# A hybrid encoder step on one core: two more gate pairs as products of halves, a written engine order ahead of them, sample logits in split products, and mask and maximum as one operation

## The chip, the cores and the metric

The kernel runs on one core of a Trainium2 chip. The metric is device time of one execution in microseconds (us). Engines are named as in the profile: PE (TensorE) multiplies matrices, PEld is its weight load, DVE (VectorE), ACT (ScalarE) and POOL (GpSimd) work element by element, SP (SyncE) issues most DMAs; ACT issues some. "Granted clock" is the share of TensorE's full clock that it got.

## What is computed

One step of a one-layer encoder with two parallel branches, for a prompt of 1024 tokens and a sample of 64 tokens that continues 128 cached ones. The model width is 1024, with 16 heads of 64. Cut to what matters here:

```python
z = rms_norm(x, g_pre) @ w_in          # x path, gate, q, k, v, gate, forget logits, two merge gates
xa, ga, q, k, v, gb, fl, ma, mb = jnp.split(z, ...)
ya = rg_lru(causal_conv(xa, ...), ...) * silu(ga)
logf = log_sigmoid(fl + b_f); cum = cumsum(logf)
s = einsum('qhd,khd->hqk', q, k) * HEAD_DIM ** -0.5 + cq - ck      # ck, cq: running sums of logf
p = softmax(where(kpos <= qpos, s, -inf))
yb = einsum('hqk,khd->qhd', p, v) * silu(gb)
mix = sum(sigmoid([ma, mb]) * [ya @ w_branch[0], yb @ w_branch[1]]) @ w_o
h = x + rms_norm(mix, g_post)
y = h + rms_norm(sigmoid(h @ w_ple_gate) * (pe @ w_ple_proj), g_ple)
```

Outputs are y, the new k, v and logf, and the recurrent states, for prompt and sample. Everything is float32.

## The kernel before

**Split products.** A float32 product is made of three matmuls in the format `float32r` (a rounded float32): each operand is split into a high part (a copy by ACT, `copy_act`, L80) and a low part (what is left, `sub`, L83, on DVE or POOL), and `three` (L166 to L169) adds high by high, high by low and low by high. The sample's scores and values in attention are made of plain float32 matmuls instead.

**Gate panels.** z is made of panels of 128 columns, transposed: `panel_steps` takes a panel in three chunks of 364, 364 and 360 tokens, each of eight steps (one per 128 rows of the contraction) of three matmuls, into one of two accumulators of the pool `mm`. A chunk ends with `spill`: ACT copies the accumulator to SBUF and issues the write to DRAM (L269). The queue `gates` holds 24 panels: ma, mb and gb, eight each. `fetch` (L236) issues a panel's weights on SP, `split_next` splits them, `panel` hands out the next and looks ahead by one.

**The stages, in order.**

1. Norm, transposes, v and the forget logits, in nine token blocks (to L518).
2. Two plain panels (`PLAIN = 2`), while ACT and DVE make the split sums and differences T1 to T4 of the quarters of the normed input (`split_sum`). They are used by
3. ten pairs (`quads`, function `seven`): two panels of weights are taken as a 2 x 2 matrix of quarters and multiplied by the quarters of the input in seven products instead of eight, in the manner of Strassen and Winograd (L691). `split_pair` makes the sums of weights (POOL) and splits them (ACT, DVE); `put` brings results out. Eight pairs are k and q of a pair of heads, two are x and gate panels of the recurrent branch (kind "r": results go to DRAM as they are). Between products, `between` runs a step of `running_sums` (cumulative logf, softplus of the decay) or writes keys out (`keys_out`).
4. Attention (from L828). Scores (L990, L991) of 128 queries against up to 1024 keys go to one of two PSUM tiles, `s1` for up to 512 keys and `s2` for more, one buffer each. `softmax` adds the causal mask to the last 128 columns (DVE, L968), takes the negated maximum (DVE, L970), the exponential with its sum (ACT, L972), the reciprocal (DVE, L974) and scales (POOL, L975). `turn` transposes the probabilities (PE, L1012) and splits them (ACT, DVE); `values` multiplies by v (L1036, L1037). Per pair of heads the sample does the same once (`sample_keys`, `sample_scores` L1066 to L1068, `sample_turn`, `sample_values`); its inputs come by `load_sample` (L951 to L960), v by `load_v` (L930).
5. The recurrent branch, the branch and output projections, the last norm and gate.

**What sets the order.** PE follows the program's order throughout (`tc.manual_schedule`). ACT, DVE and POOL are ordered by the framework's scheduler, except in the opening, in attention and in the recurrent branch, where the program's order holds for them too. In attention that order is made by a small planner: a clock `now` in ns runs along PE's work (`spent`), each operation of ACT, DVE and POOL is booked at a time with a cost (`book`, constants at L36 to L40), and a step of scores, turns or values is taken when its inputs are due plus `SLACK` = 600 ns; if none is, one step of a gate panel fills the gap (`filler`, `book_split` books its weight split 5000 ns after the panel's start). What gate panels are left when attention is done run alone behind it.

## Time and profile before

| what | value |
|---|---|
| median of 3 runs | 1516.44 us (1512.67 to 1519.98) |
| profiled execution, its own time | 1513.6 us |
| its span, first to last instruction | 1511.9 us |
| mean granted clock of TensorE | 0.988 |
| bytes moved by DMA | 181.74 MB, 120 GB/s |

A row of the groups of instructions reads: line, engine, operation, written from read tile, partitions x elements, xcount, then busy us and mean ns of one, then the idle time before them and what ended it. A row in order of time reads: start, duration (us), engine, line, operation, count. A row of the waits reads: engine, tile and line that waited, what it waited for, us in total, times, longest.

### The profile page before, as it was taken

The page shows a single profiled execution, that of the slowest core. Times are in us where ns is not written, and L with a number is a line of the kernel's source. Part 1 is how long each engine was busy: PE and PEld are TensorE (multiplying, and loading weights), DVE is VectorE, ACT ScalarE, POOL GpSimd, SP SyncE. Part 2 cuts the span into 40 slices and gives each one's busy share as a digit, 9 for nine tenths or more (in the row PEclk, how much of TensorE's full clock was granted, in tenths as well). Part 3 has the DMA queues.
Part 4 walks back from the last instruction along what each step waited for, and adds up shares of the span by engine and source line. Part 5 has one row for each costly group of instructions (what it writes and reads, how often), then busy time and mean ns, then how long its engine had stood idle before and what let it go on. Part 6 is the DMA issues. An engine that isn't in the chain of part 4 may idle for free.

```text
span 1511.9 us, 25944 instructions
## 1 busy us (share of the span) xinstructions
PE 1462.3 (97%) x10064; PEld 1435.2 (95%) x10064; DVE 891.2 (59%) x1490; ACT 688.0 (46%) x1350; POOL 345.8 (23%) x416
## 2 busy tenths in 40 slices
PE   7999999999899999999999999989999999999998
PEld 6998999999899999999999999989999999999997
DVE  5463756644166766766676236999855554337644
ACT  4423434432155565656565325566544333324533
POOL 4010414312123322322332003556323000000001
PEclk9999999999999999999999999999999999999999
DMA  5344355553665546455451331111278544215111
GB/s 192 112 119 97 114 162 179 170 155 124 187 153 123 152 105 153 116 130 130 119 133 51 99 89 44 53 34 43 66 248 267 180 145 134 84 31 169 57 48 42
DMA packets 172951, 181.74 MB, mean 120 GB/s; under 512 B 21516, under 2 KB 148700, under 8 KB 172828
## 3 DMA queue, kind: packets, MB, share of 16 engines
q1 hardware_dynamic: 153724, 153.30, 36.7%
q10 hardware_dynamic: 19104, 26.79, 5.0%
q8 instruction: 79, 1.29, 0.4%
q14 instruction: 44, 0.36, 0.1%
HBM read 122.11 MB, written 57.93 MB: 119 GB/s over the span
## 4 chain that ended last, share of the span: by engine, by line
PE 64%; DVE 6%; ACT 3%; DMA 1%; issue 1%; POOL 1%; DVEq 0%; SPq 0%; POOLq 0%; ACTq 0%
PE acc L167 14%; PE acc L169 14%; PE acc L168 14%; PE tp L1012 4%; PE quad L691 3%; PE pv L1036 3%; PE pv L1037 3%; PE s L990 2%; PE s L991 2%; DVE u L1283 1%; DMA d_gb<-st 1%; DVE e_e L1342 1%; DVE e L1342 1%; PE tp L1636 1%; PE acc7p L169 1%
## 5 line engine op out<-in xcount | busy, mean ns | idle before, releaser
L169 PE MATMUL acc<-xh,wl 128*128 128x364 f32 (+1 forms) x864 | 286.4, 332 | 6.9 <-DVE wl L83 6.9
L167 PE MATMUL acc<-xh,wh 128*128 128x364 f32 (+1 forms) x864 | 287.0, 332 | 3.5 <-ACT st L80 3.5
L168 PE MATMUL acc<-xl,wh 128*128 128x364 f32 (+1 forms) x864 | 285.8, 331 | 0.0
L169 PEld LDWEIGHTS acc<-xh,wl 128*128 128x128 f32 x864 | 164.6, 190 | 7.5 <-DVE wl L83 7.5
L167 PEld LDWEIGHTS acc<-xh,wh 128*128 128x128 f32 x864 | 165.2, 191 | 4.7 <-ACT st L80 4.1
L168 PEld LDWEIGHTS acc<-xl,wh 128*128 128x128 f32 x864 | 164.7, 191 | 0.4
L83 DVE TENSOR_TENSOR wl<-wraw,wh 128x1024 fp32r<-128x1024 f32 (+1 forms) x82 | 96.6, 1177 | 109.7 <-ACT wh L80 109.3
L80 ACT ACTIVATE wh<-wraw 128x1024 fp32r<-128x1024 f32 (+1 forms) x82 | 77.8, 949 | 91.8 <-PE quad L691 44.4
L975 POOL TENSOR_SCALAR pb<-pb,sm 128x896 f32<-128x896 f32 (+1 forms) x64 | 61.6, 963 | 192.8 <-DVE sm L974 188.9
L970 DVE TENSOR_REDUCE nm<-s 128x1 f32<-128x128 f32 (+8 forms) x136 | 99.6, 732 | 3.8
L80 ACT ACTIVATE th<-tp 128x512 fp32r<-128x512 f32 x96 | 56.1, 594 | 51.5 <-PE tp L1012 47.9
L83 DVE TENSOR_TENSOR tl<-tp,th 128x512 fp32r<-128x512 f32 x96 | 65.3, 687 | 17.0 <-ACT th L80 16.0
L990 PE MATMUL s<-k,q 128*128 128x256 f32 (+1 forms) x192 | 66.5, 350 | 8.1 <-ACT pm L972 8.1
L80 ACT ACTIVATE st<-acc 128x364 f32<-128x364 f32 (+1 forms) x72 | 33.8, 471 | 87.9 <-PE acc L169 67.1
L167 PE MATMUL acc<-wqh,hth 128*128 128x256 f32 x256 | 73.1, 285 | 0.0
L167 PE MATMUL acc<-wqh,mxh 128*128 128x256 f32 x256 | 72.6, 283 | 0.0
L168 PE MATMUL acc<-wql,mxh 128*128 128x256 f32 x256 | 72.5, 283 | 0.0
L168 PE MATMUL acc<-wql,hth 128*128 128x256 f32 x256 | 72.5, 283 | 0.0
L169 PE MATMUL acc<-wqh,mxl 128*128 128x256 f32 x256 | 72.5, 283 | 0.0
L169 PE MATMUL acc<-wqh,htl 128*128 128x256 f32 x256 | 72.5, 283 | 0.0
L972 ACT ACTIVATE pb<-s,nm 128x896 f32<-128x896 f32 (+1 forms) x64 | 61.0, 954 | 18.8 <-DVE nm L970 10.1
L691 PE MATMUL quad<-xh,wh 128*128 128x272 f32 x320 | 68.3, 295 | 0.4 <-ACT p__3650 L80 0.4
(506 smaller groups left out, 4171.5 us busy)
## 6 DMA issues: line engine op xcount, KB each, us to landing
wraw<-in_w_in SPq DMA_DIRECT2D x58, 512.0 KB
q<-d_q SPq DMA_DIRECT2D x48, 256.0 KB
k<-d_k SPq DMA_DIRECT2D x48, 256.0 KB
wraw<-in_w_branch SPq DMA_DIRECT2D x16, 512.0 KB
gate<-d_ma SPq DMA_DIRECT2D x8, 544.0 KB
yb_in<-d_y SPq DMA_DIRECT2D x8, 544.0 KB
gb_in<-d_gb SPq DMA_DIRECT2D x8, 544.0 KB
gate<-d_mb SPq DMA_DIRECT2D x8, 544.0 KB
```

Source lines behind the costliest of these rows:

```text
L80: act.activation(out=out, in_=in_, func=AF.Copy, scale=scale)
L83: return eng.tensor_tensor(out=out, in0=in0, in1=in1, op=ALU.subtract)
L167: pe.matmul(out, ah, bh, start=start, stop=False)
L168: pe.matmul(out, ah, bl, start=False, stop=False)
L169: pe.matmul(out, al, bh, start=False, stop=stop)
L691: pe.matmul(acc[:, c, :CW], l[:, k, :], r[:, k, c * CW:(c + 1) * CW], start=(first and k == 0 and p == 0), stop=(k == 3 and p == 2), skip_ ...
L970: at = book("D", at - HOP, per(D_MAX, n), lambda: dve.tensor_reduce(out=nm, in_=s[:, :n], axis=AX.X, op=ALU.max, negate=True))
L972: free = book("A", at, per(A_EXP, n), lambda: act.activation(out=pr[:, :n], in_=s[:, :n], func=AF.Exp, bias=nm, accum_out=sm))
L975: return free, book("G", at, per(G_NORM, n), lambda: pool.tensor_scalar(out=pr[:, :n], in0=pr[:, :n], scalar1=sm, scalar2=1.0, op0=ALU.mul ...
L990: pe.matmul(s[:, c0:c0 + w], t["q1"][:, q0:q0 + P], t["k1"][:, c0:c0 + w], start=True, stop=False)
L1012: pe.transpose(tp[:, o0 + i * P:o0 + (i + 1) * P], pr[par][:, kb * P:(kb + 1) * P], ident[:, :])
L1036: pe.matmul(pv[:, :256], v, th[:, c], start=(g == 0 and j == 0), stop=False)
```

## The change

- `MORE = 2`: the last four panels of `gates` (gb 4 to 7) are taken off the queue and become two more pairs of kind "r", twelve pairs in all. 18 panels stay for attention's fill instead of 22. The weights of even pairs are loaded into `wpool`, those of odd pairs into `sp_`, the other way round than before.
- Ahead of the pairs ACT and DVE follow a written order: the chunks of the two plain panels, halves of the splits T2 and T4, and the parts of the first pair's split alternate. The first operations of `running_sums` are pinned to their place in the program.
- The sample's k and q parts are written as high and low parts like the prompt's (`put`, tensors `d_k`, `d_q` of T columns) and its scores are three `float32r` matmuls and a fourth, of six rows, for all running-sum terms (`cs_q`, `cs_k`), instead of three float32 ones.
- `softmax`: mask and maximum are one DVE operation over all columns (`tensor_tensor_reduce`); it writes the negated masked scores back to PSUM. The mask tile becomes 128 x 1024, zero but for its last 128 columns, and moves from the constants to attention's pool.
- `load_v` loads and splits half a pair's values at a time; the planner's costs follow.

```diff
@@ constants and queues
+MORE = 2
-D_MASK, D_MAX, D_INV, ... = (100.0, 1.35), (155.0, 1.045), 160.0, ...
+D_MAX, D_INV, ... = (240.0, 1.05), 160.0, ...
+    some += [gates.pop() for _ in range(2 * MORE)]
-    quads += [[(src, ("r", dst)) for src, dst in some[i:i + 2]] for i in (0, 2)]
+    quads += [[(src, ("r", dst)) for src, dst in some[i:i + 2]] for i in range(0, len(some), 2)]
+    n_gates = len(gates)
...
+    def split_half(x, t, j):
+        x_, h_, l_ = (halves(y)[j] for y in (x, *t))
+        copy_act(h_, x_)
+        sub(dve, l_, x_, f(h_))
...
+        elif b == NBLK - 1:
+            plain_1 = panel()
...
-    split_sum(rc, *T3)
-    whole(rc, 1, 0)
-    sub(dve, rc, rc, ra)
-    split_sum(ra, *T2)
-    split_sum(rc, *T4)
-    r23.close()
...
-        pl = (sp_, wpool)[i % 2]
+        pl = (wpool, sp_)[i % 2]
...
+    seq = tc.manual_schedule(engines={act.engine, dve.engine})
+    seq.__enter__()
+    steps = gate_panel(*plain_1)
+    chunk(steps)
+    split_sum(rc, *T3)
+    whole(rc, 1, 0)
+    sub(dve, rc, rc, ra)
+    split_half(ra, T2, 0)
+    chunk(steps)
+    split_half(ra, T2, 1)
+    plain_2 = panel()
+    split_half(rc, T4, 0)
+    run(steps)
+    split_half(rc, T4, 1)
+    r23.close()
...
     first_split = split_pair(0, pairs[0], first_w)
-    steps = gate_panel()
-    for i in range(3 * KT):
-        next(steps)
-        if i in (7, 15):
-            next(first_split)
+    steps = gate_panel(*plain_2)
+    next(first_split)
+    chunk(steps)
+    next(first_split)
+    chunk(steps)
+    next(first_split)
     run(steps)
-    steps = gate_panel()
-    for i in range(3 * KT):
-        next(steps)
-        if i in (3, 11, 19):
-            next(first_split)
-    run(steps)
-    run(first_split)
-    pairs.append(load_pair(1))
+    next(first_split)
     split_sum(rb, *T1)
     r1.close()
+    run(first_split)
+    seq.__exit__(None, None, None)
+    pairs.append(load_pair(1))
@@ attention: set-up
-    qs = p2.tile([P, P], F32, name="qs")
-    pool.memset(qs[:, :], 0.0)
+    mask = p2.tile([P, SEQ], F32, name="mask")
+    pool.memset(mask[:, :], 0.0)
+    pool.affine_select(out=mask[:, SEQ - P:], in_=mask[:, SEQ - P:], compare_op=ALU.is_ge, fill=NEG, ...)
+    qs = [p2.tile([P, P], F32R, name=f"qs{i}") for i in "hl"]
+    cs_q = p2.tile([6, P], F32R, name="cs_q")
+    cs_k = p2.tile([6, LS], F32R, name="cs_k")
...
@@ load_v
-    def load_v(p):
-        raw = p2.tile([P, NBLK, P], F32, name="v_raw", tag="v_raw", bufs=1)
+    def load_v(p, i, tag="v_raw"):
+        raw = p2.tile([P, SEQ if tag == "pb" else SEQ // 2], F32, name=tag, tag=tag, ...)
...
@@ load_sample
-        sp.dma_start(t["ckr"][:, :], d_cs[1, 2 * p:2 * p + 2, :])
-        sp.dma_start(t["cqr"].rearrange("o (h t) -> o h t", h=2), d_cs[0:1, 2 * p:2 * p + 2, PAST:])
-        sp.dma_start(t["ks"][:, PAST:], d_ks[p])
-        for j in range(2):
-            js = slice(j * HD, (j + 1) * HD)
-            sp.dma_start(qs[js, js], d_qs[p][js, :])
+        sp.dma_start(f(cs_k[2:, :]), d_cs[2 * p:2 * p + 2].rearrange("h s t -> (h s) t"))
+        sp.dma_start(f(cs_q[:2, :]).rearrange("s (h t) -> s h t", h=2), d_cq[:, 2 * p:2 * p + 2, :])
+        for i in range(2):
+            sp.dma_start(f(t["ks"][i][:, PAST:]), d_k[i, p][:, SEQ:])
+            for j in range(2):
+                js = slice(j * HD, (j + 1) * HD)
+                sp.dma_start(f(qs[i][js, js]), d_q[i, p][js, SEQ:])
...
@@ softmax
-        at = book("D", now[0] + HOP_PE, per(D_MASK, n - d0), lambda: dve.tensor_tensor(
-            out=s[:, d0:n], in0=s[:, d0:n], in1=m, op=ALU.add))
-        at = book("D", at - HOP, per(D_MAX, n), lambda: dve.tensor_reduce(
-            out=nm, in_=s[:, :n], axis=AX.X, op=ALU.max, negate=True))
+        at = book("D", now[0] + HOP_PE, per(D_MAX, n), lambda: dve.tensor_tensor_reduce(
+            out=s[:, :n], in0=s[:, :n], in1=m, scale=-1.0, scalar=-NEG, op0=ALU.add, op1=ALU.min, accum_out=nm))
         free = book("A", at, per(A_EXP, n), lambda: act.activation(
-            out=pr[:, :n], in_=s[:, :n], func=AF.Exp, bias=nm, accum_out=sm))
+            out=pr[:, :n], in_=s[:, :n], func=AF.Exp, scale=-1.0, bias=nm, accum_out=sm))
...
@@ sample_scores
-        pe.matmul(s[:, :LS], qs[:, :], t["ks"][:, :], start=True, stop=False)
-        pe.matmul(s[:, :LS], head_of[:, :], t["ckr"][:, :], start=False, stop=False)
-        pe.matmul(s[:, :LS], t["cqr"][:, :], ones[:1, :LS], start=False, stop=True)
-        spent(1270.0)
+        three(s[:, :LS], *(x[:, :] for x in qs + t["ks"]), True, False)
+        pe.matmul(s[:, :LS], cs_q[:, :], cs_k[:, :], start=False, stop=True)
+        spent(440.0)
...
@@ go
-            if i == units[x][1] and x % UP == 3 and x // UP + 1 < NP:
-                load_v(x // UP + 1)
+            if i == units[x][1] and x % UP in (3, 5) and x // UP + 1 < NP:
+                load_v(x // UP + 1, x % UP // 4)
```

140 lines of the change are left out of this document (72 added, 68 removed).

## The prediction

> **What bounds the kernel now.** I read the page first, then the span cut into stages by windows, then TensorE's waits, then the instructions around each wait.
>
> ```profile
> span 1511.9 us, 25944 instructions
> PE 1462.3 (97%) x10064; PEld 1435.2 (95%) x10064; DVE 891.2 (59%) x1490; ACT 688.0 (46%) x1350; POOL 345.8 (23%) x416
> ```
>
> TensorE (PE) is busy 97% of the span and no other engine passes 59%. So the time is TensorE's work plus the places where TensorE stands or runs slowly. The stages show where those are; the columns are stage, its length, then busy time and count of PE, PEld, DVE, ACT and POOL, then the granted clock, the DMA share and GB/s.
>
> ```profile
> 130.70:163.45 32.75, 27.49 (x150) 26.98 (x149) 24.43 (x50) 18.23 (x28) 8.10 (x8) 0.90 0.36 78
> 163.45:388.20 224.75, 222.54 (x1777) 220.86 (x1778) 120.30 (x170) 83.82 (x181) 66.43 (x57) 1.00 0.52 160
> 388.20:421.30 33.10, 25.01 (x143) 24.63 (x142) 5.99 (x12) 6.38 (x13) 5.28 (x8) 0.90 0.69 172
> 421.30:843.65 422.35, 422.35 (x2857) 405.62 (x2856) 287.31 (x654) 247.37 (x577) 124.58 (x177) 1.00 0.49 121
> 843.65:893.40 49.75, 49.49 (x299) 49.19 (x299) 5.32 (x5) 11.12 (x18) 0.95 (x6) 1.00 0.39 104
> 950.00:1095.00 145.00, 132.77 (x769) 131.33 (x768) 133.80 (x91) 84.40 (x123) 75.08 (x76) 0.96 0.16 45
> ```
>
> From 130.70 to 163.45 lie the two plain gate panels ahead of the pairs; then ten pairs of products of halves up to 388.20; then attention, whose gaps TensorE fills with plain gate panels, up to 843.65; then gate panels alone up to 893.40. In attention TensorE is never idle while DVE has 287 of 422 us, so a shorter softmax cannot end attention work sooner than TensorE's sum allows: it only moves panels from inside attention to behind it. From 950 to 1095 DVE is the bound (133.8 of 145.0); the change leaves that stage alone.
>
> TensorE's waits in the two stages at clock 0.90:
>
> ```profile
> PE acc L167 <- ACT st L80: 3.2, 1, 3.2
> PE quad L691 <- DVE wl L83: 2.0, 1, 2.0
> PE s L990 <- ACT pm L972: 8.1, 1, 8.1
> ```
>
> Behind the long ones TensorE gets half its clock for a while:
>
> ```profile
> 138.80:142.00 3.20, 0.00 (x0) 0.00 (x0) 3.20 (x3) 3.17 (x5) 0.00 (x0) 0.90 0.32 77
> 142.00:148.60 6.60, 6.58 (x23) 6.58 (x24) 6.60 (x7) 2.04 (x4) 0.00 (x0) 0.53 0.59 104
> 417.87:421.30 3.43, 3.43 (x12) 3.43 (x13) 2.09 (x6) 1.86 (x5) 1.25 (x2) 0.51 0.98 216
> ```
>
> **Term 1: four panels become two pairs.** A plain panel is 24 steps of three matmuls; a pair is seven products of 24 matmuls, 168 in all.
>
> ```profile
> 360.20 21.08 PE quad L691 x168
> 388.19 0.33 PE L167 MATMUL acc<-xh,wh 128*128 128x364 f32 x1
> 400.13 0.33 PE L167 MATMUL acc<-xh,wh 128*128 128x364 f32 x1
> ```
>
> A pair takes 21.08 us, a panel 400.13 - 388.19 = 11.94 us. Two pairs for four panels: 4 x 11.94 - 2 x 21.08 = 5.6 us less. The panels that leave are the last four of the queue, and those are just what stands alone behind attention now: 49.75 / 11.94 = 4.2 panels. So attention keeps its 18 panels of fill. The new pairs' splits, spills and loads are like those of the present gate pairs, in a stage where DVE (120.3 of 224.8), ACT and the DMA have room; without that cover a pair waits like the last one does now, under 1 us. I take **-5.6 us** (bounds -6 and -4).
>
> **Term 2: the order ahead of the pairs.** The stage is 32.75 us long and holds 2 x 11.94 = 23.9 us of matmuls: 8.9 us are lost: 3.2 and 2.05 waiting, 3.1 in the 6.6 us at clock 0.53, the rest at the seams. What TensorE waits for at 138.8 is two accumulator copies that stand on ACT behind the splits of T3 and T2:
>
> ```profile
> 137.35 2.11 ACT L80 ACTIVATE t3h<-rc 128x1088 fp32r<-128x1088 f32 x2 [1.08 <-DVE fl L423]
> 139.37 2.09 ACT L80 ACTIVATE t2h<-ra 128x1088 fp32r<-128x1088 f32 x2
> 141.49 0.84 ACT L80 ACTIVATE st<-acc 128x364 f32<-128x364 f32 x2
> ```
>
> With the order written out, ACT does: copy of chunk 0 (at 136.8, behind the last value copies), T3 (2.1 us), half of T2 (1.05), copy of chunk 1 (near 140.4), half of T2, the first half of T4, copy of chunk 2. TensorE has two accumulators; chunk 2 can start at 138.8 and the second panel's chunk 0 at 142.7, without a wait. Its chunk 1 needs the copy of chunk 2, which is queued behind T4's first half, and that waits for DVE: T3 low (2.5), the sum and the difference of rc (2.42 each) from 138.5 on end at 145.8; half of T4 ends at 146.9, the copy at 147.4. TensorE is ready at 146.7: a wait of 0.7 us. The a11 split comes at about 151 to 152, ahead of the first product at 155.5. The small operations of the running sums, of which DVE runs some thirty there now, go behind the pairs' first products:
>
> ```profile
> 147.99 0.23 DVE L154 TENSOR_SCALAR ls_s<-ls_e 128x144 f32<-128x144 f32 x1
> 160.91 0.17 DVE L665 TENSOR_SCALAR nsp<-neg 128x8 f32<-128x8 f32 x1
> ```
>
> There they can delay a u3 or a put; I charge 0.5 us (0 to 3). POOL's four sums for the first pair keep their place; the pair's weights now land in a pool whose buffers are free earlier. Term 2: 8.9 - 1.0 = **-7.9 us**, +0.5 (bounds -9 and -2: at the upper end the new wait passes 3 us and brings back the half clock).
>
> [...]
>
> **Term 3: sample scores.** Now three f32 matmuls of 192 columns, each issued as two; then four fp32r ones.
>
> ```profile
> 531.67 0.49 PE L1066 MATMUL s<-ks,qs 128*128 128x192 f32 x2
> 532.94 0.66 PE L1012 MATMUL tp<-ident,pb 128*128 128x128 f32 x4
> 533.35 0.36 PE L1036 MATMUL pv<-diag0h,vv 128*128 128x256 f32 x1
> 537.15 0.28 PE L990 MATMUL s<-k,q 128*128 128x256 f32 x1
> 537.27 0.28 PE L991 MATMUL s<-k,q 68*128 68x256 f32 x1
> ```
>
> Three take 532.94 - 531.67 = 1.27 us, 0.42 each. No row shows an fp32r matmul under 256 columns. From below: 256 columns take 0.12 and 364 take 0.166 (three in a step of 0.497), so 192 would be 0.09 by the slope; four 128-column transposes took 0.41, 0.10 each though only half as wide, which looks like a floor per weight load. From above: the f32 rate, 0.42 each, 1.69 for four. I take 0.105, nearest to both neighbours of the right form: 0.42 for the four, 8 x (1.27 - 0.42) = **-6.8 us** (bounds -7.3 and +3.4). The added low half of the keys is one 128-column DVE operation a pair, beside other work.
>
> **Term 4: softmax.** Mask and maximum are now two DVE operations; the new one has no row on PSUM, but its kind stands at the end of the kernel, and a plain two-input operation of that size beside it:
>
> ```profile
> 555.03 0.30 DVE L968 TENSOR_TENSOR s<-s,mask 128x128 f32<-128x128 f32 x1 [0.42 <-PE s L991]
> 555.37 1.22 DVE L970 TENSOR_REDUCE nm<-s 128x1 f32<-128x1024 f32 x1
> L1788 DVE CUSTOM_DVE_ANT_0 lo7s<-ple 128x256 f32<-128x256 f32 x4 | 1.7, 424 | 0.1
> L1742 DVE TENSOR_TENSOR ple<-acc7p,ple 128x256 f32<-128x256 f32 x4 | 1.7, 422 | 5.5 <-ACT ple L1735 5.5
> L1788 DVE DVE_READ_ACCUMULATOR2_ANT ss<- 128x1 f32 x4 | 0.3, 81 | 0.0
> ```
>
> 424 against 422 ns: one pass over the elements, plus 81 ns to read the accumulator. At 1024 columns 1.22 + 0.08 = 1.30 us for 0.34 + 1.22 = 1.56: some 0.2 us less in each of 136 chains. Since TensorE is the bound there, this is worth **0 us** by itself: attention takes less fill and a panel or so is left behind it, which also covers the loads of the next stage. If it all stayed inside, up to 5 us at attention's end would lie open (0 to +5). [...]
>
> **Term 5: the wait at attention's start.** TensorE stands 8.07 us there, then runs 3.43 us at half clock.
>
> ```profile
> 404.98 2.31 SPq L960 DMA_DIRECT2D qs<-d_qs x2
> 407.40 1.16 SPq L236 DMA_DIRECT2D wraw<-in_w_in x2
> 414.41 1.06 ACT L80 ACTIVATE wh<-wraw 128x1024 fp32r<-128x1024 f32 x1 [9.61 <-DMA wraw<-in_w_in]
> 417.36 0.37 ACT L972 ACTIVATE pm<-s,nm 128x128 f32<-128x128 f32 x1 [1.89 <-DVE nm L970]
> 417.87 0.58 PE L990 MATMUL s<-k,q 128*128 128x256 f32 x1 [8.09 <-ACT pm L972]
> ```
>
> The third gate panel's weights are issued on SP behind the first sample loads; they land near 414.4, ACT's split stands in its written order ahead of the first exponential, and the next scores wait for that. The change leaves this order alone and puts more in front: the value load in two, two key loads for one, four query loads for two, 13 issues for 9. At 0.35 to 0.5 us each that is **+1.8 us** (0 to +5, the upper end if one more of them takes the long form that the two took at 404.98).
>
> **Sum.** -5.6 - 7.9 + 0.5 - 6.8 + 0 + 1.8 = -18.0 us. The profiled execution took 1513.6 us, 1.7 more than its span and 2.8 under the median of 1516.44; from it, 1495.6, and on the median's footing **1498 us**, 1.2% less. A measurement of this kernel tells about 0.5% from no change.
>
> **Rivals.** *Short fp32r matmuls run at the f32 rate* (18%). For it: the scores take 256 columns where 128 are needed, and no row goes below 256; against it: the 0.10 of the transposes. Then term 3 is +3.4 instead of -6.8: 1508 us, on the edge of "same". *The written order moves the wait instead of removing it* (14%): T4's first half is late by some 3 us, the copy of chunk 2 behind it holds TensorE past 3 us, and the clock halves again; some 6 us come back: 1504 us. So would it if the change did not do what it says there. *The combined operation is slow on PSUM* (10%), the slower side. If it took two cycles an element, the wide scores, whose single PSUM tile passes from TensorE to DVE to ACT and back, would each be about 832 x 1.04 = 0.87 us later. There are 64 of them; the plan of the order leaves 0.6 us of slack after each step, so TensorE would stand 64 x 0.27 = 17 us at least and 64 x 0.87 = 55 at most, and there is no fill left to hide it: 1515 to 1553, say 1535. It decides from about 0.9 us of delay a wide score if the slack holds, 0.3 if not. Against it: the 424 ns above, and the mask row, which reads and writes PSUM at one pass (0.30 for 128 columns).
>
> **How the numbers follow.** Forecast 58%, rivals 18, 14 and 10. Term by term the forecast's own range is 1490 to 1505; with the first two rivals, and without the slower one, 1488 to 1512. Faster by over 0.5% (under 1508.9): the forecast, the second rival and half of the first, less a little for what I have not seen: 0.78. Within 0.5%: 0.12. Slower: 0.10.
>
> **What would show it.** The stage of the two plain panels should be about 25 us long, with no wait over 1 us and clock 1.0 throughout. The pairs should be twelve, about 267 us. Sample scores should follow each other at about 0.1 us a matmul. The combined operation at 1024 columns should read about 1.3 us with its accumulator. The wait behind the first exponential should be near 10 us. Behind attention one or two gate panels should stand alone instead of four; none, with TensorE idle there, would be wrong. The prediction fails if TensorE has new idle inside attention, or if the short matmuls read 0.3 us or more.

## The result, and the profile after

The changed kernel takes 1519.13 us (median of 20 runs, 1513.68 to 1520.94), the kernel before 1514.37 us (20 runs, 1511.98 to 1519.98). The ratio is 1.0026 with a 95% interval of 1.0016 to 1.0035: no gain, and if anything 4 us lost, where 18 us of gain were forecast. The profiled execution took 1520.73 us.

The head of the page after. TensorE has 2 us less to do, in a span 7 us longer:

```profile
span 1519.0 us, 26162 instructions
PE 1460.3 (96%) x10096; PEld 1433.4 (94%) x10096; DVE 877.1 (58%) x1516; ACT 688.4 (45%) x1343; POOL 360.8 (24%) x443
```

To see where, I cut both executions at the same events of TensorE: the first plain panel ahead of the pairs, the first product, the end of the products, the ninth row of score matmuls, the last attention matmul, the first gate matmul of the recurrent branch, the end of its work. First the windows of before, then those of after (length, busy time and count of PE, PEld, DVE, ACT, POOL, granted clock, DMA share, GB/s):

```profile
130.70:160.75 30.05, 26.83 (x146) 26.54 (x145) 21.76 (x45) 15.53 (x23) 8.10 (x8) 0.89 0.36 83
160.75:388.20 227.45, 223.20 (x1782) 221.30 (x1782) 122.97 (x175) 86.52 (x186) 66.43 (x57) 1.00 0.52 159
388.20:422.19 33.99, 25.90 (x149) 25.52 (x147) 5.99 (x12) 6.38 (x13) 5.87 (x9) 0.90 0.70 173
422.19:844.51 422.32, 422.32 (x2857) 405.60 (x2857) 287.31 (x654) 247.84 (x578) 123.98 (x175) 1.00 0.49 121
844.51:904.36 59.85, 59.59 (x361) 59.29 (x360) 13.03 (x11) 13.40 (x22) 2.85 (x12) 1.00 0.36 98
904.36:1504.41 600.05, 585.83 (x4052) 583.08 (x4051) 374.88 (x468) 273.19 (x444) 116.16 (x125) 0.99 0.33 103
```

```profile
128.78:152.60 23.82, 23.82 (x147) 23.82 (x145) 15.84 (x15) 11.64 (x16) 5.96 (x8) 1.00 0.37 65
152.60:430.76 278.16, 268.35 (x2117) 266.33 (x2117) 149.60 (x223) 99.41 (x197) 81.45 (x73) 0.99 0.51 150
430.76:467.65 36.89, 26.46 (x149) 26.08 (x147) 5.43 (x12) 6.39 (x13) 6.26 (x11) 0.86 0.65 158
467.65:892.31 424.66, 420.37 (x2827) 402.88 (x2827) 257.92 (x662) 246.88 (x577) 128.24 (x193) 0.99 0.50 120
892.31:907.39 15.08, 14.17 (x87) 13.87 (x86) 6.58 (x7) 3.50 (x6) 2.02 (x8) 1.00 0.41 112
907.39:1511.41 604.02, 588.16 (x4051) 584.86 (x4051) 375.50 (x469) 273.97 (x446) 115.45 (x125) 0.99 0.33 103
```

Set against the forecast, with the terms laid on these cuts (the first product was forecast at 155.5; the 2.0 us wait of before lies just behind its first product):

| stage | before | after | change | forecast |
|---|---|---|---|---|
| up to the first product | 160.8 | 152.6 | -8.2 | -5.2 |
| pairs | 227.4 | 278.2 | +50.7 | 42.16 - 2.05 + 0.5 = +40.6 |
| attention's start | 34.0 | 36.9 | +2.9 | +1.8 |
| attention | 422.3 | 424.7 | +2.3 | -6.8 there, |
| from its end to the first gate matmul | 59.9 | 15.1 | -44.8 | -47.8 here |
| recurrent branch and the rest | 600.1 | 604.0 | +4.0 | 0 |

The gain ahead of the pairs is there and more. Then 10 us are lost in the pairs, 9 in attention (the stage got longer by 2.3 although TensorE's work in it is less), 3 behind it, 4 in the recurrent branch. The waits of TensorE from the plain panels to the first gates name the places:

```profile
PE s L1016 <- ACT pm L998: 10.4, 1, 10.4
PE quad L704 <- ACT p__1579 L82: 4.7, 1, 4.7
PE quad L704 <- DVE u__3463 L799: 2.5, 1, 2.5
PE s L1016 <- ACT pb L998: 1.7, 1, 1.7
PE pv L1062 <- DVE y L1071: 1.5, 1, 1.5
```

Here `pm` and `pb` are the exponentials of narrow and wide scores; `p__`, `u__` and `qo` are the copies, sums and outputs that empty the products' accumulators in the pairs; `st`, below, is a spill buffer. In before only the first of these waits was there (8.1), and the third with 0.84. The theory that I tested (**A**): each part saves what its operations promise, and the saving is handed back at a later instruction that waits for a late DMA. The rivals: the two new pairs cost more than the panels (**B**), the written order (**C**) or the combined operation (**G**) is what hurts.

### The profile page after: what moved, and what is told of

Its sections match the earlier page's. It is cut to its first block, busy times and chain, and to the rows that moved or that the text cites. A ratio compares the mean times of both kernels' runs of the same rounds, so it can differ in the third digit from the quotient of the medians.

```text
span 1519.0 us, 26162 instructions
## 1 busy us (share of the span) xinstructions
PE 1460.3 (96%) x10096; PEld 1433.4 (94%) x10096; DVE 877.1 (58%) x1516; ACT 688.4 (45%) x1343; POOL 360.8 (24%) x443
## 4 chain that ended last, share of the span: by engine, by line
PE 71%; DVE 9%; DMA 9%; ACT 5%; issue 3%; POOL 2%; SPq 1%; ACTq 0%; DVEq 0%; POOLq 0%
PE quad L704 14%; PE acc L158 11%; PE acc L160 11%; PE acc L159 11%; PE tp L1038 4%; DMA wraw<-in_w_in 3%; PE pv L1062 2%; PE pv L1063 2%; PE s L1016 2%; PE s L1017 2%; DMA gb_in<-d_gb 1%; PE vacc L158 1%; PE vacc L159 1%; PE vacc L160 1%; DMA d_ma<-st 1%
## 5 line engine op out<-in xcount | busy, mean ns | idle before, releaser
L160 PE MATMUL acc<-xh,wl 128*128 128x364 f32 (+1 forms) x768 | 254.0, 331 | 6.8 <-DVE wl L85 6.8
L158 PE MATMUL acc<-xh,wh 128*128 128x364 f32 (+1 forms) x768 | 255.6, 333 | 0.0
L159 PE MATMUL acc<-xl,wh 128*128 128x364 f32 (+1 forms) x768 | 254.1, 331 | 0.0
L160 PEld LDWEIGHTS acc<-xh,wl 128*128 128x128 f32 x768 | 146.2, 190 | 7.4 <-DVE wl L85 7.4
L158 PEld LDWEIGHTS acc<-xh,wh 128*128 128x128 f32 x768 | 146.5, 191 | 1.1
L159 PEld LDWEIGHTS acc<-xl,wh 128*128 128x128 f32 x768 | 146.6, 191 | 0.7
L996 DVE CUSTOM_DVE_ANT_0 s<-s,mask 128x128 f32<-128x128 f32 (+7 forms) x128 | 95.6, 768 | 24.9 <-PE s L1017 24.5
L704 PE MATMUL quad<-xh,wh 128*128 128x272 f32 x384 | 82.3, 296 | 5.7 <-ACT p__1579 L82 4.7
L704 PE MATMUL quad<-xl,wh 128*128 128x272 f32 x384 | 80.0, 290 | 0.0
L1016 PE MATMUL s<-k,q 128*128 128x256 f32 (+1 forms) x192 | 68.1, 358 | 12.1 <-ACT pm L998 10.4
L704 PE MATMUL quad<-xh,wl 128*128 128x272 f32 x384 | 79.7, 289 | 0.0
L82 ACT ACTIVATE th<-tp 128x512 fp32r<-128x512 f32 x96 | 56.7, 597 | 37.3 <-PE tp L1038 34.1
```

Source lines behind the costliest of these rows:

```text
L82: act.activation(out=out, in_=in_, func=AF.Copy, scale=scale)
L158: pe.matmul(out, ah, bh, start=start, stop=False)
L159: pe.matmul(out, ah, bl, start=False, stop=False)
L160: pe.matmul(out, al, bh, start=False, stop=stop)
L704: pe.matmul(acc[:, c, :CW], l[:, k, :], r[:, k, c * CW:(c + 1) * CW], start=(first and k == 0 and p == 0), stop=(k == 3 and p == 2), skip_ ...
L996: at = book("D", now[0] + HOP_PE, per(D_MAX, n), lambda: dve.tensor_tensor_reduce(out=s[:, :n], in0=s[:, :n], in1=m, scale=-1.0, scalar=-N ...
```

## The experiments

All ratios are to the kernel before, run beside it on the same chip, with 95% intervals.

| run | what | median us | ratio, interval |
|---|---|---|---|
| e1 | after, spill in a borrowed buffer | 1512.27 | 0.9998, 0.9987 to 1.0010 |
| e2 | after, ten pairs | 1516.64 | 1.0023, 1.0012 to 1.0035 |
| e3 | after, old order ahead | 1517.96 | 1.0027, 1.0015 to 1.0040 |
| e4 | before, twelve pairs | 1519.46 | 1.0040, 1.0025 to 1.0055 |
| e5 | after, another borrowed buffer | 1514.40 | 1.0002, 0.9991 to 1.0013 |
| e6 | after, third panel early | 1503.45 | 0.9940, 0.9925 to 0.9955 |
| e7 | after, spills by GpSimd | 1504.42 | 0.9939, 0.9925 to 0.9954 |
| e8 | after, softmax in two operations | 1518.67 | 1.0035, 1.0023 to 1.0048 |
| e9 | e5 + e6 + e7 | 1503.22 | 0.9937, 0.9922 to 0.9951 |
| e10 | before + e6 + e7 | 1515.61 | 1.0017, 1.0004 to 1.0031 |
| e11 | e9, ten pairs | 1503.50 | 0.9940, 0.9922 to 0.9959 |
| e12 | e9, old order | 1507.57 | 0.9964, 0.9951 to 0.9978 |
| e13 | e5 + e6 | 1503.33 | 0.9939, 0.9919 to 0.9960 |
| e14 | before + e6 | 1502.89 | 0.9941, 0.9922 to 0.9959 |
| e15 | e13, ten pairs | 1501.96 | 0.9938, 0.9918 to 0.9958 |
| e16 | e6, three spill buffers | 1502.82 | 0.9944, 0.9924 to 0.9964 |
| e17 | e13 + later spills by GpSimd | 1495.03 | 0.9883, 0.9866 to 0.9900 |
| e18 | e14 + later spills by GpSimd | 1503.93 | 0.9948, 0.9929 to 0.9967 |

### The combined operation (e8)

```diff
-        at = book("D", now[0] + HOP_PE, per(D_MAX, n), lambda: dve.tensor_tensor_reduce(
-            out=s[:, :n], in0=s[:, :n], in1=m, scale=-1.0, scalar=-NEG, op0=ALU.add, op1=ALU.min, accum_out=nm))
+        at = book("D", now[0] + HOP_PE, per((100.0, 1.35), P), lambda: dve.tensor_tensor(
+            out=s[:, n - P:n], in0=s[:, n - P:n], in1=m[:, n - P:], op=ALU.add))
+        at = book("D", at - HOP, per((155.0, 1.045), n), lambda: dve.tensor_reduce(
+            out=nm, in_=s[:, :n], axis=AX.X, op=ALU.max, negate=True))
...
-            out=pr[:, :n], in_=s[:, :n], func=AF.Exp, scale=-1.0, bias=nm, accum_out=sm))
+            out=pr[:, :n], in_=s[:, :n], func=AF.Exp, bias=nm, accum_out=sm))
```

> The changed kernel with mask and maximum as two VectorE operations again (mask added to the last 128 columns, then the maximum), the rest as changed. Forecast's term 4 and theory A (TensorE bounds attention, the combined operation is worth nothing by itself): 1519.1 +- 2 us, VectorE some 30 us busier. Rival G (the combined operation moved the order of the steps so that the issue of a spill falls into the choked stretch): the wait of the scores behind the exponential in attention's third quarter goes, 1513 to 1516 us.

1.0035 against the changed kernel's 1.0026: no difference. The groups of VectorE in attention, first in after (busy, mean ns of one), then in e8:

```profile
L996 DVE CUSTOM_DVE_ANT_0 s<-s,mask 128x128 f32<-128x128 f32 (+7 forms) x128 | 95.6, 768 | 24.9 <-PE s L1017 24.5
L996 DVE DVE_READ_ACCUMULATOR2_ANT nm<- 128x1 f32 x136 | 18.9, 139 | 0.0
```

```profile
L998 DVE TENSOR_REDUCE nm<-s 128x1 f32<-128x128 f32 (+8 forms) x136 | 99.3, 731 | 3.3
L996 DVE TENSOR_TENSOR s<-s,mask 128x128 f32<-128x128 f32 x128 | 37.3, 292 | 27.2 <-PE s L1019 26.3
```

95.6 + 18.9 against 99.3 + 37.3: the change saves VectorE some 20 us (the sample's few operations are counted on one side only), and the whole not one. The combined operation isn't slow on PSUM: at 1024 columns it takes 1.23 us, as the maximum alone does in e8 (1.22). Rival G is out: the wait of the scores for an exponential stays in e8, 1.2 us.

### The two pairs (e2, e4)

```diff
-MORE = 2
+MORE = 0
```

> The changed kernel with MORE = 0: ten pairs, and 26 panels of gates for attention and behind it, all else as changed. Theory A (a pair is worth what was forecast, 2.8 us, but the four panels behind attention had covered the loads and the start of the recurrent branch): +5.6 for the panels, -4 to -6 where the next stage starts with them as cover: 1518 to 1521 us. Rival B (pairs beyond ten cost more than two panels each, by waits of their own): -5 to -11, 1508 to 1514 us. Forecast's own terms: 1519.1 + 5.6 = 1524.7.

> The kernel before with the two more pairs alone. Theory A: four panels for two pairs, -5.6, but nothing is left behind attention to cover the start of the recurrent branch, +4 to +6: 1513 to 1515 us. Forecast's own term 1: 1514.4 - 5.6 = 1508.8 us. Rival B (a pair beyond ten costs more than two panels): 1516 to 1522 us.

e4 is the kernel before with the line `some += [gates.pop() for _ in range(2 * MORE)]` and the longer list of pairs. Taking the pairs out (e2, 1.0023 against 1.0026) changes nothing; adding them to the kernel before (e4, 1.0040) costs 6 us. Yet each new pair costs just what the row of a gate pair had said. ACT's first copy of each of the last three pairs in after stands 21.0 us apart:

```profile
369.77 0.63 ACT L82 ACTIVATE p__4139<-quad 128x544 f32<-128x544 f32 x1 [2.56 <-PE quad L704]
390.80 0.62 ACT L82 ACTIVATE p__4355<-quad 128x544 f32<-128x544 f32 x1 [2.56 <-PE quad L704]
411.84 0.62 ACT L82 ACTIVATE p__4575<-quad 128x544 f32<-128x544 f32 x1 [2.56 <-PE quad L704]
```

So the saving is real where it is made. By its time e4 lies in rival B's range and not in theory A's, but not for rival B's reason (new pairs with waits of their own): its tenth and eleventh pair take 21.0 us each. In e4 the saving is lost at four places, by the same cuts as above: the pairs take 3.6 us more than the two new ones (in the first and the seventh pair), the way from attention to the first gate matmul takes 43.9 us less instead of 47.8, attention's start 1.2 more, and the rest of the kernel 604.9 us instead of 600.1; the opening gained 1.9. The second and the last belong to the change: with no panel left behind attention, the recurrent branch starts against its own operands. Its first gate matmuls wait for ACT and VectorE (`uh`, 3.8 us in e4; in before they don't wait) and start at half clock (granted clock 0.95 over the last 16.03 us ahead of the first of them, where before has 1.00).

### The order ahead (e3), and the spill behind which the first copy stands (e1, e5)

```diff
-    seq = tc.manual_schedule(engines={act.engine, dve.engine})
-    seq.__enter__()
-    steps = gate_panel(*plain_1)
-    chunk(steps)
     split_sum(rc, *T3)
...
-    seq.__exit__(None, None, None)
...
-        pl = (wpool, sp_)[i % 2]
+        pl = (sp_, wpool)[i % 2]
```

> The changed kernel with the old free order of ACT and DVE ahead of the pairs (and the pairs' weights in the old two pools). Theory A: the stage ahead of the pairs is 8.9 us longer again, the third product's wait and its half clock (6.4) and a part of the pairs' later waits (0 to 3) go: 1518.5 to 1521.6 us. Rival C (the written order costs nothing in the pairs; the 4.7 is chance of the DMA): +8.9, 1528 us.

No difference: 1.0027 against 1.0026. The first product starts 6.4 us later (158.97 against 152.60), and the copy of its result is made at the same time. First in after, then in e3:

```profile
162.79 0.60 ACT L82 ACTIVATE p__1579<-quad 128x544 f32<-128x544 f32 x1
```

```profile
162.72 0.63 ACT L82 ACTIVATE p__1576<-quad 128x544 f32<-128x544 f32 x1 [0.48 <-PE quad L696]
```

What holds it in after stands on ACT in front of it:

```profile
158.34 0.47 ACT L82 ACTIVATE st<-acc 128x360 f32<-128x360 f32 x1 [7.46 <-DMA d_ma<-st]
...
159.22 0.63 ACT L82 ACTIVATE wh<-s 128x512 fp32r<-128x512 f32 x1 [0.40 <-ACT st L82]
...
160.27 2.09 ACT L82 ACTIVATE xh<-rb 128x1088 fp32r<-128x1088 f32 x2
...
```

The last spill stood 7.46 us for one of two buffers, whose write had been issued at 145.84, 1 us behind a load of the second pair's weights, and landed 12 us later. From its issue to 158.34, when the spill went on, the DMA share was 0.22, 0.47 and 0.67 (145.84 to 150, to 154, to 158.34); what held the write, no run shows. e1 and e5 give this spill a buffer of its own, out of the pool that also holds the weights of the second pair:

```diff
-        s = wpool.tile([P, GC], F32, name="st")
+        s = f(other[:, :GC]) if other is not None else wpool.tile([P, GC], F32, name="st")
...
+            tag[1], t0, n, z, sp_.tile([P, HT], F32R, name="oh", tag="oh", bufs=2) if own and c == 2 else None))
```

(in e1 the tile is `kl`, in float32 and with one buffer)

> The changed kernel, with one edit: the last spill ahead of the pairs (chunk 2 of the second plain panel) gets a buffer of its own, so that it needn't wait for the write of the chunk before last. Theory A (what was saved ahead of the pairs is given back in them, because ACT's written order holds the copy of the first product behind this spill): the 4.7 us wait of the third product and the some 1.7 us of half clock behind it go, 1519.1 - 6.4 = 1512.7 us. Rival (the copy is late because of the T1 splits or of POOL and DVE sharing, not of the spill): the wait stays over 3 us and the time stays at 1519.

> As e1_third_buffer, but the borrowed buffer is one of the two that hold the high halves of outputs (first wanted again some 10 us later than the buffer borrowed there, for which VectorE stood 4.0 us until the write had landed). Theory A (a write that lands 12 us late holds whoever wants its buffer next, and only that): the 4.7 us wait and the 4.1 us wait of e1 are both gone, no wait over 2 us before the pairs' middle; 1519.1 - 6.4 - 0 to 4 (the wait behind u3 in e1 was borrowed, so it isn't in the changed kernel) = 1509 to 1513 us. Rival D (the running sums behind the first products are what is late there, since they stand in VectorE's queue): a wait of 2 us or more behind u3 stays, 1512 to 1516 us.

By ratio they are 4.2 and 3.6 us faster than the changed kernel, where theory A expected 6.4. In both the copy now comes at 157.3, and the wait of the third product is gone. But something else is late: in e1 VectorE stood 4.0 us for the borrowed buffer, whose write landed 13 us after its issue, and TensorE 4.1 us behind u3; in e5, where that is gone, TensorE stands 3.0 us for `qo`, and in e13, with the same edit, 3.6 us. In e13 GpSimd's first sum for the second pair, which starts that chain:

```profile
167.25 1.29 POOL L560 TENSOR_TENSOR s<-wraw 128x512 f32<-128x512 f32 x1 [32.31 <-DMA wraw<-in_w_in]
```

SP issued these weights from 144.85 on; they were used at 167.25, 22 us later, and the splits on ACT and VectorE and then VectorE's sum for `qo` queued behind them. Against rival D (the running sums are what is late) speaks that VectorE stood idle 4.9 us in e13 ahead of the split of these weights. But this wait was brought in by the edit itself. SP's first issue for the second pair, in after and then in e13:

```profile
125.42 0.37 SPq L537 DMA_DIRECT2D wraw<-in_w_in  x1
```

```profile
144.85 0.99 SPq L538 DMA_DIRECT2D wraw<-in_w_in  x2
```

The borrowed buffer stands in the pool ahead of the weights and moves them to places that come free later: in after the first load goes out when a write of v has landed, in e13 this one and the next go out only after the split of T2. In after GpSimd's sum starts at 160.65 and waits for VectorE, not for weights. So e1, e5 and every run with e5's edit trade one late DMA for another; the first copy of the second pair comes at 184.25 in after, 184.30 in e3 and 184.97 in e13. e16, further down, gives the spill a third buffer without moving the weights.

### The start of attention (e6, e14)

```diff
     while owed:
         owed.popleft()[1]()
     split_next(dve)
+    fetch(*choose())
     psq.close()
```

> The changed kernel with the weights of attention's third panel fetched ahead of the first head's and sample's loads. Theory A (the wait at attention's start is the weights' late landing, behind 22 issues on SP's queue): the 10.4 us wait falls under 3 us and the half clock behind it goes: 1519.1 - 8 to 12 = 1507 to 1511 us. Rival E (the scores would wait anyway, for the first head's rows or for the copies that follow): the wait stays over 6 us or the first scores come later, 1514 to 1519 us.

> The kernel before with the edit of e6 alone. Theory A2 (the 8.1 us wait and the 3.4 us at half clock go here too, about 10 us, and e10 hid it by GpSimd's late spills): 1503 to 1506 us; then the whole change is worth 5 us with this wait out of both (e13 against e14), not the forecast 18. Rival J (the change made the wait at attention's start its own bill, and before gains little from the edit): 1510 to 1514 us.

The largest bill of all, and the change didn't make it. In after the third panel's weights land behind 21 issues of SP (the expectation miscounted one); ACT waits 12.28 us for them with the exponential behind:

```profile
459.66 1.06 ACT L82 ACTIVATE wh<-wraw 128x1024 fp32r<-128x1024 f32 x1 [12.28 <-DMA wraw<-in_w_in]
```

In e6 the same stretch, from the last product to the ninth row of scores, takes 24.16 us instead of 36.89, with TensorE never idle and at full clock; the whole gained some 4 us more than the most that was expected:

```profile
427.30:451.46 24.16, 24.16 (x148) 24.07 (x147) 5.60 (x12) 6.50 (x13) 6.02 (x10) 1.00 0.69 174
```

The kernel before gains 9 us from the same line (e14, 0.9941) and the changed one 13, so rival J is out. And it sets e13 against e14: with this wait out of both, the whole change was worth nothing (1503.33 and 1502.89), where 5 us were expected.

### What the sample scores saved in attention (e7, e9 to e13, e15, e16)

The scores themselves. Four matmuls from 471.50 to 472.19, 0.69 us against 1.27 before, the same in all eight places: 4.6 us saved. The first two steps take 0.09 and 0.11 us, as forecast; from the third matmul to the one of six rows it takes 0.21, and from that to the next matmul 0.28.

```profile
471.50 0.25 PE L158 MATMUL s<-ksh,qsh 128*128 128x192 f32 x1
...
471.91 0.35 PE L1094 MATMUL s<-cs_k,cs_q 6*128 6x192 f32 x1
472.19 0.43 PE L158 MATMUL acc<-xh,wh 128*128 128x364 f32 x1
```

But attention has new stops, 4.3 us of idle TensorE (424.66 - 420.37) where before had none, and about 3 us more by half clock behind the wait for `pb` (granted clock 0.50 from 758 to 764). Around that wait, in after, SP and then ACT:

```profile
745.84 6.01 SPq L916 DMA_DIRECT2D k<-d_k  x2
```

```profile
751.30 0.47 ACT L82 ACTIVATE st<-acc 128x364 f32<-128x364 f32 x1 [1.91 <-PE acc L160]
754.88 0.33 ACTq L266 DMA_DIRECT2D d_mb<-st  x1
755.25 0.28 ACT L82 ACTIVATE pts<-tps 128x128 f32<-128x128 f32 x1 [3.48 <-DMA wraw<-in_w_in]
755.43 1.00 ACT L998 ACTIVATE pb<-s,nm 128x896 f32<-128x896 f32 x1
```

ACT ended a spill at 751.77 and could issue its write only at 754.88, while SP took 6 us to issue two loads; the exponential came at 755.43. What ACT waited for stands in its next row: a panel's weights, which SP had issued at 740.24 and which landed at 754.80. The spill doesn't need them, and its write went out 0.08 us after they had landed. SP stood for ACT's writes too: at the start of attention in after 5.5 and 2.5 us, until two spills had landed. In before SP's issues at the same head took 2.8 us, ACT's spill went out at 705.47, ahead of the jam, and TensorE waited for nothing. e7 takes the issue off ACT:

```diff
-        act.dma_start(dst[:, t0:t0 + n], s[:, :n])
+        (by or act).dma_start(dst[:, t0:t0 + n], s[:, :n])
...
-                    spill(dst, t0, n, z)
+                    spill(dst, t0, n, z, by=pool)
```

> The changed kernel with the spills of attention's gate panels issued by GpSimd instead of ScalarE. Theory A (in attention's third quarter ScalarE stands 3 to 5 us at the issue of a spill while the DMA queues are choked, the exponential behind it is late, and TensorE waits 1.7 to 4 us and then has half its clock for some 7 us): that wait and the half clock go, -4 to -5 us; the issues cost GpSimd some 50 short stops, which nobody waits for: 1514 to 1515 us. Rival F (the exponential is late for another reason, or the scores only wait for the rows of the next head): 1519 us, with a wait of over 1.5 us at the same head.

0.9939, 13 us faster than the changed kernel and three times what was expected. Attention from the ninth row on took 416.85 us instead of 424.66 with no wait for an exponential, its start 5 us less (the wait there was 5.2 us instead of 10.4), the pairs 5 us less, which is no work of this edit. At the start SP no longer waits for spills, and from its first load for attention to the third panel's weights it took 15.0 us instead of 20.5. e9 to e12 put the edits together.

> The changed kernel with the edits of e5, e6 and e7 together: the spill ahead of the pairs in a buffer of its own, the third panel's weights ahead of attention's first loads, attention's spills issued by GpSimd. Theory A (three separate waits behind late DMAs ate what the change saved; e6 and e7 share a part, since both shorten the start of attention): 1489 to 1497 us, no wait over 3 us from the pairs to attention's end. Rival H (the waits only pass on: what attention gains is lost at the start of the recurrent branch, which has its own loads to wait for): 1500 to 1505 us, as e6 and e7 alone.

> The kernel before with the two edits that apply to it: the third panel's weights ahead of attention's first loads, attention's spills issued by GpSimd. Theory A (the change itself is worth what its parts saved, about 8 ahead of the pairs, 5.6 for the pairs and 4.6 for the sample scores, 18 us, once the late DMAs are out of the way): 1514 - 8 to 12 = 1502 to 1506, and 10 to 18 us over e9. Rival I (the edits alone made the gain and the change adds nothing): within 4 us of e9.

> e9 with MORE = 0: ten pairs and four plain panels more. Theory A (term 1 is worth up to 5.6 us, less what the four panels hide behind attention): 2 to 6 us over e9. Rival B (a pair beyond ten costs more than two panels, whatever the waits): 0 to 8 us under e9.

> e9 with the old free order ahead of the pairs (the edit of e5 doesn't apply to it). Theory A (the written order is worth 7.9 us where nothing is given back in the pairs): 5 to 9 us over e9. Rival C2 (the order moves the waits of the opening and of the pairs about, and is worth 0 to 3): within 3 us of e9, with a new wait ahead of the plain panels or in the pairs in either.

The edits didn't add up (e9, 0.9937, where 1489 to 1497 us were expected), and in before (e10) they brought nothing: the start of attention took 33.5 us in e9 and 33.1 in e10, as if the third panel had not been fetched early. There GpSimd's first issues stand behind its copies of v, the spills land late, and ACT stands up to 7.4 us (e9) and 8.1 us (e10) for a spill buffer. That is the same fault once more, of my own making. e11 shows the pairs worth nothing here either, where 2 to 6 us were expected; e12 gives the written order 4 us, 5 to 9 expected (0.9964 against 0.9937, the intervals touch).

> The changed kernel with the edits of e5 and e6, without that of e7. In e9 GpSimd's issues of the first spills stood behind its value copies, the writes landed late, and ScalarE stood 7 us for a spill buffer with an exponential behind it. Theory A2 (each stop is a spill that waits for a buffer whose write is late; the two edits are in separate stages and add up): 1503.5 - 4 to 5 = 1498 to 1500 us, the start of attention without a wait as in e6. Rival H (whatever is gained ahead of the recurrent branch is lost at its start): 1503 us, with TensorE idle 3 us or more between attention and the first gates.

> e13 with MORE = 0. Theory A2 (term 1: two pairs for four panels are worth 5.6 us, less the 2 to 5 that four panels behind attention hide of the recurrent branch's start): 1 to 4 us over e13. Forecast's term 1: 5.6 over e13. Rival B (the pairs beyond ten bring waits of their own): 0 to 5 under e13.

> The changed kernel with the edit of e6 and three spill buffers for the whole kernel instead of two (the separate small buffer of the key outputs goes, and one of three output buffers in attention). Theory A2: the spill's waits go ahead of the pairs as in e13 and in attention's third quarter as well: 1494 to 1499 us. Rival K (in attention ScalarE stands at the issue, not for a buffer, and a third buffer doesn't help there): as e13, 1498 to 1500, with the scores' wait of 1.5 us or more behind the exponential still there.

e13 (without the edit of e7) has the start at 24.1 us, but attention at 424.89, and is no faster than e6: rival H's time, though not by rival H, since from attention's end to the first gate matmul it took 14.6 us, as e6. e15: two pairs more or less, no difference, where theory A2 expected 1 to 4 us. e16 is inconclusive on the third buffer in attention: to make room one of three buffers of `y` went, and TensorE waited 6.4 us for `y`; the wait of the scores for `pb` stayed (2.5 us), as rival K said. Ahead of the pairs it decides. The weights of the second pair go out at 124.78, as in after, the first copy comes at 157.41, and the second pair's at

```profile
177.88 0.62 ACT L82 ACTIVATE p__1858<-quad 128x544 f32<-128x544 f32 x1 [1.14 <-PE quad L704]
```

6.4 us earlier than in after, where theory A had expected 6.4 from e1. The first pair takes 21.6 us in e16, 28.1 in after and 27.9 in e13. So the spill's buffer accounts for the loss there.

### Both waits out (e17, e18)

```diff
-                    spill(dst, t0, n, z)
+                    spill(dst, t0, n, z, by=pool if now[0] > 60000.0 else act)
```

> e13, with GpSimd issuing attention's spills only from 60 us of planned time on, so that the start of attention stays as in e6. Theory A3 (what the sample scores save, 4.6 us, is lost in attention to ScalarE's stops at the issue of spills; in e7, without them, attention from its eighth score matmul on took 416.9 us, in e13 424.9): the start takes 24 us from the last product to the eighth pair of score matmuls, the rest of attention 417 to 420 us: 1496 to 1499 us. Rival L (the next stage takes back whatever attention gains): 1502 to 1505 us, with the time from the first gate matmul to the end 4 us longer or more.

> The kernel before with the early third panel and GpSimd issuing the later spills. Theory A3 (the kernel before has no stop of that kind in attention, 422.3 us there in e14, no wait of the scores behind an exponential): as e14, 1502 to 1505 us, so the whole change is worth 4 to 8 us against e17. Rival I (the edit is good for both alike and the change is worth nothing): within 2 us of e17.

This decides it. e17 takes 1495.03 us, 0.9883 (0.9866 to 0.9900): faster than both kernels, by 1.2%. The kernel before with those of the edits that apply to it takes 1503.93 (e18), no better than e14. Their runs don't overlap (four from 1491.42 to 1496.10, six from 1501.32 to 1509.44), and their profiles have the cuts to show it. First e17, then e18, from the pairs on:

```profile
152.60:421.80 269.20, 265.02 (x2118) 263.20 (x2116) 146.68 (x223) 99.72 (x197) 81.04 (x73) 1.00 0.50 157
421.80:446.00 24.20, 24.20 (x149) 24.11 (x148) 5.63 (x12) 6.51 (x13) 5.62 (x9) 1.00 0.72 174
446.00:863.30 417.30, 416.62 (x2827) 400.20 (x2826) 258.05 (x662) 246.65 (x577) 155.71 (x236) 1.00 0.52 126
863.30:879.00 15.70, 14.18 (x88) 13.88 (x86) 6.61 (x7) 3.53 (x6) 3.00 (x13) 1.00 0.39 104
878.97:1486.30 607.33, 590.74 (x4051) 587.62 (x4051) 374.69 (x469) 274.16 (x446) 115.04 (x125) 0.98 0.32 103
```

```profile
157.70:386.60 228.90, 224.19 (x1781) 222.71 (x1781) 125.33 (x178) 86.52 (x186) 67.44 (x57) 0.99 0.51 159
386.60:410.80 24.20, 24.20 (x149) 24.11 (x148) 5.99 (x12) 6.50 (x13) 3.83 (x6) 1.00 0.68 172
410.80:833.20 422.40, 422.40 (x2858) 405.47 (x2857) 286.92 (x654) 248.72 (x578) 152.25 (x223) 1.00 0.50 125
833.20:894.20 61.00, 59.77 (x361) 59.17 (x360) 13.04 (x11) 12.96 (x22) 10.18 (x25) 1.00 0.34 95
894.18:1496.38 602.20, 587.85 (x4052) 584.80 (x4051) 375.40 (x468) 273.44 (x444) 116.17 (x125) 0.99 0.32 103
```

With these waits out, the change is worth: -5.1 us up to the first product (152.6 against 157.7); +40.3 for two pairs, less than their 42.0; nothing at the start; -5.1 in attention, where the sample scores save 4.6; -45.3 behind it, where four panels are 47.8; and +5.1 in the recurrent branch. In all -10.1 us between the profiles, -8.9 between the medians, half of the forecast 18. The 2.5 us lost behind attention and 3.7 of the 5.1, which lie in the recurrent branch's first gate matmuls (6.7 us for the first 18, 3.0 in e18), are what two pairs cost by leaving no panel there; the last 1.4 have no cause shown. The +40.3 is partly chance: the first pair took 23.5 us in e17, and 27.9 in e13, which has the same program up to there.

## Why the prediction was wrong, by its own steps

The step that failed is the one that adds the five terms up: it takes what each saves on TensorE straight off the time, as if nothing else came due behind it. The runs showed spills, weights and the next stage's start coming due there, and these took back all of it.

**Term 1** priced the pair rightly (21.0 us) and the panel too. What failed is the step "the panels that leave ... are just what stands alone behind attention now: 49.75 / 11.94 = 4.2 panels", costed as 47.8 us of TensorE's time. They were cover as well: with twelve pairs the recurrent branch starts 2.5 to 4 us late, and its first 18 gate matmuls take 4.3 us at full clock (after, e13) and 6.0 and 6.7 where they start at half clock (e4, e17; granted clock 0.56 in the first 4 us of e17); with panels ahead of them they take 3.0 in each of seven profiles. The term came out between 0 (e2, e11, e15) and +6 (e4). The prediction had named this cover in term 4 ("also covers the loads of the next stage") and left it out of term 1, where it was used up.

**Term 2** got its stage right, 23.8 us with no wait and clock 1.0, and failed on both sides of it. The 8.9 us that it set out to remove were mostly those of one execution: in the four other profiles with the opening of before (e4, e10, e14, e18) the two panels take 24.1 to 25.1 us instead of 30.0, without the 3.2 us wait and its half clock. There TensorE waits 1.8 to 3.7 us for copies of v ahead of the panels, a wait that the old order has in e3 and e12 too and the written one in no profile, and the first product starts at 156.0 to 158.9, not 160.8. So the order is worth some 5 us up to there (the middle one of the five is at 157.7). Behind it, the 0.5 us charged for later were for the running sums; the rival "moves the wait" was put on T4's first half and 6 us of return. The place was another: the last spill, for a buffer whose write was late. Of the 8.2 us at the first product, 3.6 are left at the second pair's first copy: 187.9 in before, 184.3 in after. In e16, with a third buffer, it comes at 177.9.

**Term 3** was mis-sized: 0.69 us for four, not 0.42, because the fourth is slower than the three; 4.6 us, not 6.8, inside the bounds. The step that failed with it is that this comes straight off the time. In after it was lost to the stops in attention, and it came back with them out: 417.3 us against 422.4.

**Term 4** was right: nothing, and the operation's time near the forecast 1.3 us (1.23 at 1024 columns, and 0.14 for its accumulator). **Term 5** was right in size (the start took 2.9 us more, 1.8 forecast), but stood in the wrong place of the argument: a 10 us wait was taken as given and its growth priced, when one load moved in front of the others removes it.

The rivals: the short `float32r` matmuls don't run at the f32 rate (the first two steps take 0.09 and 0.11 us, where the f32 ones took 0.42), and the combined operation isn't slow on PSUM (1.23 us at 1024 columns, the maximum alone 1.22). The slower side came by a mechanism that wasn't among them, though all its rows were in the trace of before: ACT waits for `d_ma<-st` there too (4.0 us at 150.41), and such waits cost nothing as long as TensorE isn't behind them.

**Open.** The loss at the recurrent branch's first gates comes in each of the 13 profiles with twelve pairs (1.3 to 3.7 us), but in the whole of the branch it can vanish: e13 with twelve pairs has 601.7 us there and e15 with ten 601.6. In after ACT's write at 754.88 went out 0.08 us behind the landing of SP's weights; why it stood for them, no run shows. Why SP's two issues take 3.7 and 2.3 us is not explained. Ten pairs were not run with the edits of e17, nor e17 with the spill buffer of e16.

## What to carry to other kernels

When an instruction is put earlier, ask which DMA it now outruns: here, with TensorE at 97%, the next bound was not an engine; it was a write that must land before a buffer is free (ACT stood 7.46 us for one in after), or an issue that stood until an unrelated DMA had landed (in after it went out 3.1 us behind its spill's end and 0.08 us behind that landing). Look at more than one profile before a wait is priced: the largest one ahead of the pairs stood in one of five. Check that an edit which adds a buffer moves no other tile. Work that stands alone behind a stage is also the cover of the next stage's start, so its removal has a price on both sides. And before a long wait is priced as given, see whether one load ahead of the others takes it away: here that one line was worth 9 us in the kernel before, as much as the whole change at its best.

## What the runs showed of the hardware

The shorter of two idle times of TensorE was the one followed by half clock. In after, 1.71 us without work ahead of 756.57 were followed by what adds up to 6.8 us at half clock; in e1, 3.21 us at the same place of the program, ahead of 755.07, by none. The windows around both (start and end, length, busy time and count of PE, PEld, DVE, ACT and POOL, granted clock, DMA share, GB/s), first after, then e1:

```profile
754.86:756.57 1.71, 0.00 (x1) 0.00 (x0) 0.02 (x1) 1.32 (x4) 0.00 (x0) 1.00 1.08 283
756.57:758.00 1.43, 1.43 (x5) 1.19 (x6) 0.67 (x3) 1.41 (x5) 1.12 (x2) 0.82 1.01 241
758.00:760.00 2.00, 2.00 (x9) 1.69 (x9) 2.00 (x5) 0.56 (x3) 0.36 (x1) 0.50 0.97 267
760.00:764.00 4.00, 4.00 (x16) 3.77 (x17) 2.24 (x8) 2.10 (x6) 1.71 (x2) 0.50 0.37 112
764.00:766.00 2.00, 2.00 (x12) 1.87 (x11) 0.03 (x1) 0.47 (x1) 0.00 (x0) 0.92 0.00 0
```

```profile
751.00:754.00 3.00, 0.86 (x6) 0.56 (x4) 0.00 (x0) 0.25 (x2) 0.00 (x0) 1.00 1.03 293
754.00:757.00 3.00, 1.93 (x10) 1.56 (x10) 1.19 (x4) 2.48 (x8) 1.47 (x2) 1.00 0.99 252
757.00:760.00 3.00, 2.88 (x19) 2.56 (x19) 2.72 (x9) 2.16 (x4) 0.00 (x0) 1.00 0.53 166
760.00:763.00 3.00, 3.00 (x22) 2.79 (x21) 2.12 (x6) 1.28 (x5) 1.68 (x2) 1.00 0.30 94
```

So the length of these two waits alone doesn't tell what they cost in clock; why the one in after was followed by half clock and the one in e1 was not, no run here shows.
